# Prompt attention of a hybrid decoder layer: queries of the dilated patterns read in place, with a column step, instead of gathered into tiles

## The chip, the cores and the metric

The kernel runs on one core of one Trainium2 chip and computes one whole decoder layer for a prompt of 2048 tokens and for 64 sample tokens. The metric is device microseconds of one execution of the program. The median of three runs of the kernel before is 2801.09 us (2798.26 to 2801.12). Differences below about 0.2% can't be told from no change.

## The reference

The layer has two mixers side by side (attention in three dilated patterns, and a gated linear attention), a projection, and a feed-forward part with a convolution. Only the prompt attention matters here. Each of 8 heads (64 wide) attends in three patterns: window 128 and dilation 1, window 512 and dilation 4, window 2048 and dilation 16. Positions are split by their residue modulo the dilation, so that each pattern is a band of width 128 on strided subsequences. The three outputs are merged with weights proportional to their softmax denominators.

```python
PATTERNS = ((128, 1), (512, 4), (2048, 16))

def dilated_prompt(q, k, v, window, dil):
    ...
    n = window // dil
    span = n * dil
    ...
    def to_blocks(t):
        ...
        t = t.reshape(B, nb, n, dil, H, E)
        return t.transpose(0, 3, 4, 1, 2, 5)
    ...
    s = jnp.einsum('brhcie,brhcje->brhcij', qb, kk) * (E ** -0.5)
    ...
    s = jnp.where(mask, s, NEG)
    lse = jax.nn.logsumexp(s, axis=-1)
    p = jnp.exp(s - lse[..., None])
    o = jnp.einsum('brhcij,brhcje->brhcie', p, vv)
    ...

def prompt_attn(q, k, v):
    return combine_patterns([dilated_prompt(q, k, v, w, d) for w, d in PATTERNS])
```

## The kernel before

The program has three stages: the projections (`sweeps`), the prompt attention (`attention`), and the output projection with the feed-forward part (`tail`). The projections leave queries and keys in device memory, each split into a high and a low part (`qh`, `ql`, `kh`, `kl`), the queries in natural order of position, the keys in an order in which every block needed later consists of runs of 8 or 32 neighbouring columns.

`attention` goes through four pairs of heads. For each pair it walks the patterns 0, 1 and 2, and in each pattern four groups `g`. A group holds four blocks of 128 queries. In patterns 0 and 1 a group is two units of two blocks, in pattern 2 it is one unit of four blocks; so a pair has 20 units. For a pair, the tiles `aqs` (queries, one for each head, high and low part on the two halves of the partitions), `akh` and `akl` (keys) hold all 2048 positions; they come from two pools that alternate from pair to pair, and `at_load` fetches the next pair's on the SP queue while the present one is worked on. `at_loadv` fetches the values (`av`), also on SP.

A unit (`AtUnit`) has three steps. `qk_` computes the scores: for each block and head two matmuls into `pas`, with the queries as the stationary operand and 128 or 256 keys (high, then low part) as the moving one; DVE adds the mask and takes the row minimum (L1825; the queries carry a factor of -1/8), ACT takes the exponential (L1829). `t` transposes the weights on PE into `pat` (L1846), and ACT or DVE copies them to `apt` (L61, L63). `pv` multiplies with the values into `pao` (L1863), and DVE copies a finished group to `aop`. `drain` lets `t` run two units and `pv` three units behind `qk_`. The order on PE is fixed by `line` in `AtUnit`: each matmul is ordered behind the one recorded before.

In pattern 0 the 128 queries of a block are neighbours, and the stationary operand is a plain slice of `aqs`. In pattern 1 a block takes every 4th position, in pattern 2 every 16th. For these, `at_gather` copies the queries of a whole group, per head, into a tile `aqg` of 128 x 512 on POOL (L1128), two groups before they are used; there are five such tiles in the ring. `at_operands` then takes a slice of `aqg`.

When a pair's last unit is done, `at_merge` weights and adds its three patterns. It is a generator, moved on by one step per group of the next pair. Its bulk runs on POOL: for each of four column blocks, three multiplications of `aop` with the weights `awb` (L1227), two additions (L1212, L1237) and a store (L1239), behind DMAs that bring the weights in broadcast form (L1197, L1185). `aop` has five buffers, so that pattern 2 of the next pair is written into the buffer of this pair's pattern 0. The gathers and the merge stand in one fixed order on POOL, set by `Layer.line` (L1116); POOL executes it in order. The last pair is merged on PE, DVE, ACT and POOL together.

Of the kernel before, what the change touches and what calls it, by code (L numbers as in the profile page):

```python
# [11 lines left out]
F32R = mybir.dt.float32r  # L12
# [20 lines left out]
def cap(ap, off, dims):  # L33
    return bass.AP(tensor=ap.tensor, offset=ap.offset + off, ap=[list(ap.ap[0])] + [list(d) for d in dims])


class Layer:
# [369 lines left out]
    def sweep_a(self, c):  # L407
# [39 lines left out]
        for nn in range(2):  # L447
            wv = [self.wget(), self.wget()]
            for t0, m in self.vblocks(c):
                ps = self.psum.tile([128, 512], F32, name=self.n("pv"), tag="g1", bufs=3)  # L450
                self.vgemm(ps, xs, t0, m, wv)
                vs = self.st.tile([128, 256], F32, name=self.n("vs"), tag="vs", bufs=self.AB["vsb"])
                self.evac(vs[:m], ps[:m, :256], "v")
# [502 lines left out]
        yield  # L956


    AB = dict(mw=1, qg=5, vsb=5, mq='p', klh=1, q=2, v=6, s=6, pt=4, op=5, ps=3, ppt=2, po=2, am=1, skew=(2, 3), man=(), ea=3, ed=5, mp=12, aa=(1, 4, 7, 9, 10), ms='pppp', mv=2, em=1)

    def px(self, name, dt=F32):
        return self.pxpool.tile([128, 2 * H], dt, name=self.n(name), tag="px", bufs=4)
# [22 lines left out]
    def attention(self):  # L985
        with ExitStack() as ctx:
            self.aq[1] = self.pool(ctx, "at1")
            p = self.ap = self.pool(ctx, "at")
            self.app = self.pool(ctx, "atp", bass.MemoryType.PSUM)
            self.ev = 0  # L990
            pend = None
            fifo = []
            sk = self.AB["skew"]

            def drain(n):
                nonlocal pend
                if len(fifo) > sk[0]:
                    fifo[-1 - sk[0]].t()
                while len(fifo) > n:
                    un = fifo.pop(0)  # L1000
                    un.t()
                    un.pv()
                    if un.last:
                        for _ in pend or ():
                            pass
                        pend = self.at_merge(un.pr, un.ML, un.OP)

            if self.AB['man']:
                eng = mybir.EngineType
                ctx.enter_context(self.tc.manual_schedule(engines={getattr(eng, e) for e in self.AB['man']}))  # L1010
            self.vq = []
            self.at_loadv(0)
            self.at_loadv(1)
            for _ in self.at_load(0, ((1, 2),), to=self.qk0):
                pass
            rest = self.at_load(0, ((2, 4),), to=self.qk0)
            self.qgn = []
            for _ in range(self.AB["qg"]):
                p.tile([128, 4, 128], F32R, name=self.n("aqg"), tag="aqg", bufs=self.AB["qg"])
            for pat in range(3):  # L1020
                for _ in range(2):
                    p.tile([128, 16, 4], F32, name=self.n("aml"), tag=f"aml{pat}", bufs=2)
            for _ in range(2):
                p.tile([128, 3, 4, 128], F32, name=self.n("awb"), tag="awb", bufs=2)
            for _ in range(2):
                p.tile([128, 512], F32, name=self.n("amo"), tag="amo", bufs=2)
            pre = iter(())
            for pr in range(4):
                if pr == 3:
                    self.rctx.close()  # L1030
                    pre = self.wo_pre()
                qk = self.qk0
                nxt = self.at_load(pr + 1) if pr < 3 else iter(())
                ML, OP = [], []
                for pat in range(3):
                    base = 16 * (3 * pr + pat)
                    ml = p.tile([128, 16, 4], F32, name=self.n("aml"), tag=f"aml{pat}", bufs=2)
                    op = p.tile([128, 4, 512], F32, name=self.n("aop"), tag="aop", bufs=self.AB["op"])
                    ML.append(ml)
                    OP.append(op)  # L1040
                    for g in range(4):
                        if base // 4 + g + 2 < 48:
                            self.at_loadv(base // 4 + g + 2)
                        for _ in rest:
                            pass
                        po = [None]
                        nu = 1 if pat == 2 else 2
                        for u in range(nu):
                            fifo.append(AtUnit(self, pr, pat, g, u, nu, qk, base, ML, OP, po))
                            fifo[-1].qk_()  # L1050
                            drain(sk[1])
                            if pat:
                                next(pre, None)
                        if pend is not None:
                            next(pend, None)
                        if 5 <= 4 * pat + g < 11:
                            self.qk0 = next(nxt, self.qk0)
            for _ in pre:
                pass
            drain(0)  # L1060
            for _ in pend:
                pass
# [33 lines left out]
    def at_operands(self, qk, h, pat, g, blk):  # L1096
        QS, KH, KL = qk
        q, K = QS[h], (KH[h], KL[h])
        if pat == 0:
            idx = g * 4 + blk  # L1100
            lq = q[:, 128 * idx:128 * idx + 128]
            off = g * 512 + 8 * blk
            pst = 8 if blk else 488
            if idx == 0:
                return lq, [cap(k, off, [[32, 16], [1, 8]]) for k in K], [0], idx
            return lq, [cap(k, off - pst, [[pst, 2], [32, 16], [1, 8]]) for k in K], [idx - 1, idx], idx
        lq = self.qg[h][:, blk, :]
        if pat == 1:
            idx = g * 4 + blk
            if blk == 0:  # L1110
                return lq, [cap(k, 32 * g, [[128, 4], [1, 32]]) for k in K], [idx], idx
            return lq, [cap(k, (blk - 1) * 512 + 32 * g, [[512, 2], [128, 4], [1, 32]]) for k in K], [idx - 1, idx], idx
        idx = 4 * g + blk
        return lq, [cap(k, 32 * idx, [[512, 4], [1, 32]]) for k in K], [idx], idx

    def line(self, ins):  # L1116
# [2 lines left out]
            self.after(ins, self.atpo)  # L1119
        self.atpo = ins  # L1120
        return ins

    def at_gather(self, qk, pat, g):
        qg = []
        for h in range(2):
            t = self.ap.tile([128, 4, 128], F32R, name=self.n("aqg"), tag="aqg", bufs=self.AB["qg"])
            src = cap(qk[0][h], g, [[512, 4], [4, 128]]) if pat == 1 else cap(qk[0][h], 4 * g, [[1, 4], [16, 128]])
            self.line(self.nc.gpsimd.tensor_copy(t, src))  # L1128
            qg.append(t)
        self.qgn.append(qg)  # L1130

    def at_merge(self, pr, ML, OP):
        nc, p, pp, AB = self.nc, self.ap, self.app, self.AB
# [651 lines left out]
class AtUnit:  # L1785
# [13 lines left out]
    def qk_(self):  # L1799
        L = self.L  # L1800
        nc, p1, pp, AB = L.nc, L.aq[1], L.app, L.AB
        nbk = 4 // self.nu
        self.s = []
        if self.u == 0:
            if self.pat:
                L.qg = L.qgn.pop(0)
            n = 4 * self.pat + self.g + 2
            if 4 <= n < 12:
                L.at_gather(self.qk, n // 4, n % 4)
        scores = []  # L1810
        for h in range(2):
            ps = pp.tile([128, 512], F32, name=L.n("pas"), tag="as", bufs=AB["ps"])
            info = []
            scores.append((ps, info))
            for bb in range(nbk):
                lq, rk, keys, idx = L.at_operands(self.qk, h, self.pat, self.g, self.u * nbk + bb)
                nk = 128 * len(keys)
                sc = bb * (512 // nbk)
                for z in range(2):
                    self.line(nc.tensor.matmul(ps[:, sc:sc + nk], lq, rk[z], start=(z == 0), stop=(z == 1)))  # L1820
                info.append((self.u * nbk + bb, idx, sc, nk, keys))
        for h, (ps, info) in enumerate(scores):
            ssb = p1.tile([128, 512], F32, name=L.n("ass"), tag="ass", bufs=AB["s"])
            for blk, idx, sc, nk, keys in info:
                red = nc.vector.tensor_tensor_reduce(  # L1825
                    ssb[:, sc:sc + nk], ps[:, sc:sc + nk], L.amk[self.pat][:, 256 - nk:256],
                    scale=1.0, scalar=3e38, op0=ALU.add, op1=ALU.min, accum_out=self.ml[:, idx, h:h + 1])
            for blk, idx, sc, nk, keys in info:
                ex = nc.scalar.activation(ssb[:, sc:sc + nk], ssb[:, sc:sc + nk], AF.Exp, bias=self.ml[:, idx, h:h + 1],  # L1829
                                     scale=-1.0, accum_out=self.ml[:, idx, 2 + h:3 + h])  # L1830
            L.atl = ex, red
            self.s.append((ssb, info))
# [183 lines left out]
```

## Time and profile before

One execution was recorded by the profiler; times inside it count from the start of its span. PE is TensorE's matmuls and PEld its weight loads, DVE is VectorE, ACT is ScalarE, POOL is GpSimd, SP the engine that issues most DMAs.

| what | us |
|---|---|
| median of three runs | 2801.09 |
| span of the profiled execution | 2804.5 |
| first score matmul of the attention stage | 785.06 |
| first weight load of the output projection behind it | 1103.14 |
| first score load from `aqg` (pair 0, pattern 1) | 820.10 |
| POOL busy with the gathers (64 CASTs at L1128) | 69.0 |

The span is 3.4 us longer than the median of the runs. In the answers of the trace a row of a group reads: line, engine, operation, tile written <- tiles read, size x count, then busy time, mean ns of one, and the idle time before it with what ended it. In a timeline row the first two numbers are the start in us and the length in us. A table of stretches gives for each the busy time of each engine with its count of instructions, the granted TensorE clock (1.00 is full), the DMA share and GB/s.

### The profile page before, as it was taken

How to read it: one execution, taken by the hardware profiler on the slowest of the kernel's cores; microseconds unless marked ns; L12 is line 12 of the kernel's file. 1: busy time of each engine (PE TensorE's matmuls, PEld its weight loads, DVE VectorE, ACT ScalarE, POOL GpSimd, SP SyncE). 2: the span in 40 equal slices, each digit the busy share in tenths (PEclk: the TensorE clock that was granted, in tenths of full speed). 3: DMA queues.
4: the chain of work that ended last, by engine and by line, in shares of the span. 5: the costliest groups of instructions: out<-in, count | busy, mean ns of one | idle time of the engine just before them, and what ended most of it. 6: DMA issues, size and time to landing. Idle time of an engine off the chain costs nothing. (4 is left out here: it accounts for less than half of the span.)

```text
span 2804.5 us, 58656 instructions
## 1 busy us (share of the span) xinstructions
PE 2693.6 (96%) x22267; PEld 2540.2 (91%) x22267; DVE 1841.5 (66%) x4578; ACT 1267.8 (45%) x2959; POOL 590.0 (21%) x741
## 2 busy tenths in 40 slices
PE   7999999999989998998999999999999999999997
PEld 6788898888778787998899998999999999999997
DVE  6666655444347677466998888676567765666666
ACT  6535433333358776344554444443244433443332
POOL 3424243333333666013000012000020000200001
PEclk9999999999989989999999999999999999999998
DMA  7745536689798865367577677886598875876654
GB/s 293 259 173 178 177 108 215 253 328 374 262 222 171 190 159 152 106 216 261 192 276 287 232 261 291 287 298 236 204 330 282 297 244 200 324 255 215 221 188 149
DMA packets 283595, 656.83 MB, mean 234 GB/s; under 512 B 31841, under 2 KB 81633, under 8 KB 281265
## 3 DMA queue, kind: packets, MB, share of 16 engines
q1 hardware_dynamic: 253008, 574.66, 60.7%
q0 software_dynamic: 13216, 46.56, 5.1%
q10 hardware_dynamic: 17088, 31.86, 3.1%
q8 instruction: 176, 2.88, 0.4%
q14 instruction: 107, 0.87, 0.1%
HBM read 509.02 MB, written 143.94 MB: 233 GB/s over the span
## 5 line engine op out<-in xcount | busy, mean ns | idle before, releaser
L68 ACT ACTIVATE ws<-wr 128x512 fp32r<-128x512 f32 (+1 forms) x482 | 292.6, 616 | 431.5 <-PE pfe L1588 144.3
L90 PE MATMUL pfd<-hh,ws 128*128 128x264 f32 x2816 | 477.6, 286 | 6.7 <-ACT ws L68 5.0
L90 PEld LDWEIGHTS pfd<-hh,ws 128*128 128x128 f32 x2816 | 402.3, 190 | 9.1 <-ACT ws L68 6.7
L71 DVE TENSOR_TENSOR ws<-wr,ws 128x512 fp32r<-128x512 f32 (+1 forms) x482 | 319.2, 668 | 133.5 <-ACT ws L68 130.0
L90 PE MATMUL pfd<-hl,ws 128*128 128x264 f32 x1408 | 304.3, 286 | 0.1
L1588 PE MATMUL pfa<-xh,ws 128*128 128x264 f32 x1496 | 292.7, 286 | 7.7 <-ACT ws L68 3.3
L1588 PE MATMUL pfe<-xh,ws 128*128 128x264 f32 x1496 | 289.2, 286 | 3.8 <-DVE u L1575 1.9
L1588 PE MATMUL pfd<-xh,ws 128*128 128x264 f32 x1408 | 288.3, 285 | 3.8 <-DVE up L1575 2.9
L1588 PEld LDWEIGHTS pfa<-xh,ws 128*128 128x128 f32 x1496 | 237.1, 190 | 9.7 <-ACT ws L68 3.8
L1588 PEld LDWEIGHTS pfe<-xh,ws 128*128 128x128 f32 x1496 | 236.5, 189 | 4.5 <-DMA ws<-d_wst 2.3
L398 PE MATMUL pv<-wh,xh 128*128 128x256 f32 (+1 forms) x816 | 234.7, 288 | 1.1 <-DVE th L695 1.1
L1588 PEld LDWEIGHTS pfd<-xh,ws 128*128 128x128 f32 x1408 | 231.0, 189 | 4.6 <-DVE up L1575 3.4
L398 PE MATMUL pv<-wl,xh 128*128 128x256 f32 (+1 forms) x816 | 232.3, 285 | 0.0
L398 PE MATMUL pv<-wh,xl 128*128 128x256 f32 (+1 forms) x816 | 231.6, 284 | 0.0
L90 PEld LDWEIGHTS pfd<-hl,ws 128*128 128x128 f32 x1408 | 227.5, 190 | 0.4 <-DVE hl L71 0.4
L1537 POOL DMA_DIRECT2D xl<-d_xst x52 | 28.6, 550 | 903.0 <-PE pfe L1588 872.7
L1829 ACT ACTIVATE ass<-ass,aml 128x256 f32<-128x256 f32 (+1 forms) x384 | 173.6, 454 | 88.8 <-DVE aml L1825 87.5
L1588 PE MATMUL pfd<-xl,ws 128*128 128x264 f32 x704 | 200.6, 285 | 0.0
L90 PE MATMUL pq<-xh,wh 128*128 128x512 f32 (+2 forms) x480 | 175.5, 373 | 10.4 <-ACT xh L236 8.1
L1588 PE MATMUL pfe<-xl,ws 128*128 128x264 f32 x616 | 175.7, 285 | 0.0
L1588 PE MATMUL pfa<-xl,ws 128*128 128x264 f32 x616 | 175.1, 284 | 0.0
L90 PE MATMUL pq<-xl,wh 128*128 128x512 f32 (+2 forms) x480 | 174.4, 365 | 0.0
(341 smaller groups left out, 6624.0 us busy)
## 6 DMA issues: line engine op xcount, KB each, us to landing
ws<-d_wst SPq DMA_DIRECT2D x248, 512.0 KB
wr<-in_wu SPq DMA_DIRECT2D x114, 512.0 KB
d_wst<-ws SPq DMA_DIRECT2D x88, 512.0 KB
wr<-in_wd SPq DMA_DIRECT2D x160, 256.0 KB
wr<-in_wt SPq DMA_DIRECT2D x60, 512.0 KB
wh<-d_wbs SPq DMA_DIRECT2D x35, 512.0 KB
wl<-d_wbs SPq DMA_DIRECT2D x35, 512.0 KB
skp<-in_ckt SPq DMA_DIRECT2D x16, 1024.0 KB
```

The lines of the kernel that those rows point to most:

```text
L68: h = nc.scalar.activation(hi, src, AF.Copy)
L71: return h, (nc.gpsimd if lo_eng == "p" else nc.vector).tensor_tensor(lo, src, hi.bitcast(F32), op=ALU.subtract)
L90: mm = nc.tensor.matmul(o, ww[:, k, :], xx[:, s0:s0 + n], start=(k == order[0] and i == 0), stop=(k == order[-1] and i == 2))
L398: mm = nc.tensor.matmul(ps[:m, :256], x[:, t0:t0 + m], w[:, k % 4, :], start=(k == 0 and i == 0), stop=(k == KT - 1 and i == 2))
L1537: self.nc.gpsimd.dma_start(t.bitcast(F32), xo[i, z])
L1588: self.lastmm = nc.tensor.matmul(bank[:, :H], w[:, ww, k, :], xx, start=new and k == 0 and j == 0, stop=k == 3 and j == 2, skip_group_chec ...
L1829: ex = nc.scalar.activation(ssb[:, sc:sc + nk], ssb[:, sc:sc + nk], AF.Exp, bias=self.ml[:, idx, h:h + 1], scale=-1.0, accum_out=self.ml[: ...
```

## The change

The copies into `aqg` are dropped, with the tiles and the list that held them. `at_operands` builds the stationary operand of patterns 1 and 2 as an access pattern on `aqs` itself: 128 columns with a step of 4 or of 16 elements of 4 bytes. Pattern 0, the matmuls' order and number, the softmax, the values and the merge are as they were.

```diff
-        lq = self.qg[h][:, blk, :]
         if pat == 1:
             idx = g * 4 + blk
+            lq = cap(q, 512 * blk + g, [[4, 128]])
...
         idx = 4 * g + blk
+        lq = cap(q, idx, [[16, 128]])
         return lq, [cap(k, 32 * idx, [[512, 4], [1, 32]]) for k in K], [idx], idx
...
-    def at_gather(self, qk, pat, g):
-        qg = []
-        for h in range(2):
-            t = self.ap.tile([128, 4, 128], F32R, name=self.n("aqg"), tag="aqg", bufs=self.AB["qg"])
-            src = cap(qk[0][h], g, [[512, 4], [4, 128]]) if pat == 1 else cap(qk[0][h], 4 * g, [[1, 4], [16, 128]])
-            self.line(self.nc.gpsimd.tensor_copy(t, src))
-            qg.append(t)
-        self.qgn.append(qg)
...
-        if self.u == 0:
-            if self.pat:
-                L.qg = L.qgn.pop(0)
-            n = 4 * self.pat + self.g + 2
-            if 4 <= n < 12:
-                L.at_gather(self.qk, n // 4, n % 4)
```

`cap(t, off, dims)` is an access pattern on tile `t`: offset and (step, count) pairs along the free axis. Three places of the built programs show what this does to the order of instructions; numbers behind the names are the tiles' own and differ between the two programs, and the lines of the changed file are 3 to 17 smaller.

On PE, in pair 1 at the start of a unit of pattern 1, two output matmuls of an earlier unit and the first score matmuls of this one; `aqg` is the gathered tile. Before:

```order
L1863 MATMUL pao_11066<-apt_11015,av_10683 64x128
L1863 MATMUL pao_11066<-apt_11021,av_10683 64x128
L1820 MATMUL pas_11091<-akh_9995,aqg_10889 128x128
L1820 MATMUL pas_11091<-akl_10089,aqg_10889 128x128
L1820 MATMUL pas_11091<-akh_9995,aqg_10889 128x256
L1820 MATMUL pas_11091<-akl_10089,aqg_10889 128x256
```

And after, at the same place:

```order
L1846 MATMUL pao_11009<-apt_10958,av_10642 64x128
L1846 MATMUL pao_11009<-apt_10964,av_10642 64x128
L1803 MATMUL pas_11030<-akh_9970,aqs_9880 128x128
L1803 MATMUL pas_11030<-akl_10060,aqs_9880 128x128
L1803 MATMUL pas_11030<-akh_9970,aqs_9880 128x256
L1803 MATMUL pas_11030<-akl_10060,aqs_9880 128x256
```

Order and sizes are the same; only the second operand, the stationary one, is now the pair's whole query tile.

On POOL, where the merge of pair 1 begins in pair 2 (`awt`, `awb` the merge's weights, `aop` the pattern outputs). Before:

```order
L1128 COPY aqg_11697<-aqs_10979 128x512
L1128 COPY aqg_11699<-aqs_11254 128x512
L1197 DMA d_awd<-awt_11690 96x128
L1128 COPY aqg_11793<-aqs_10979 128x512
L1128 COPY aqg_11795<-aqs_11254 128x512
L1185 DMA awb_11883<-d_awd 64x1536 x2
L1128 COPY aqg_11893<-aqs_10979 128x512
L1128 COPY aqg_11895<-aqs_11254 128x512
L1185 DMA awb_11983<-d_awd 64x1536 x2
L1227 TENSOR_TENSOR aop_10365<-aop_10365,awb_11883 128x4x128
```

And after:

```order
L1186 DMA d_awd<-awt_11621 96x128
L1174 DMA awb_11806<-d_awd 64x1536 x2
L1174 DMA awb_11902<-d_awd 64x1536 x2
L1216 TENSOR_TENSOR aop_10328<-aop_10328,awb_11806 128x4x128
L1216 TENSOR_TENSOR aop_10737<-aop_10737,awb_11806 128x4x128
```

The merge's own instructions keep their order; the copies that stood before and between them are gone.

On SP, the queue of loads at the start of pair 2: the values of pair 2 (`av`), and queries and keys of pair 3. Before:

```order
L1088 DMA av_11330<-out_o_vp 128x1x128 x4
L1088 DMA av_11400<-out_o_vp 128x1x128 x4
L1076 DMA aqs_12084<-d_qh_60 64x4x512
L1076 DMA aqs_12084<-d_ql_64 64x4x512
L1076 DMA akh_12184<-d_kh_68 64x4x512 x2
L1076 DMA akl_12282<-d_kl_72 64x4x512 x2
L1076 DMA aqs_12359<-d_ql_64 64x4x512
L1076 DMA aqs_12359<-d_qh_60 64x4x512
L1076 DMA akh_12432<-d_kh_68 64x4x512 x2
L1088 DMA av_11471<-out_o_vp 128x1x128 x4
```

And after:

```order
L1085 DMA av_11261<-out_o_vp 128x1x128 x4
L1085 DMA av_11331<-out_o_vp 128x1x128 x4
L1073 DMA aqs_11999<-d_qh_60 64x4x512
L1073 DMA aqs_11999<-d_ql_64 64x4x512
L1085 DMA av_11402<-out_o_vp 128x1x128 x4
L1073 DMA akh_12095<-d_kh_68 64x4x512
L1085 DMA av_11495<-out_o_vp 128x1x128 x4
L1073 DMA akh_12095<-d_kh_68 64x4x512
L1073 DMA akl_12189<-d_kl_72 64x4x512
```

The next pair's keys, and the second head's queries, now stand behind value loads that they stood ahead of. The first load into an `aqs` buffer waited for POOL before, for the last gather from it; now it waits for PE, for the last score matmul that reads it.

More of the change, by code (lines that the diff above doesn't have):

```diff
@@ L956, in gla_sample @@
         yield
-    AB = dict(mw=1, qg=5, vsb=5, mq='p', klh=1, q=2, v=6, s=6, pt=4, op=5, ps=3, ppt=2, po=2, am=1, skew=(2, 3), man=(), ea=3, ed=5, mp=12, aa=(1, 4, 7, 9, 10), ms='pppp', mv=2, em=1)
+    AB = dict(mw=1, vsb=5, mq='p', klh=1, q=2, v=6, s=6, pt=4, op=5, ps=3, ppt=2, po=2, am=1, skew=(2, 3), man=(), ea=3, ed=5, mp=12, aa=(1, 4, 7, 9, 10), ms='pppp', mv=2, em=1)
     def px(self, name, dt=F32):
@@ L1016, in attention @@
             rest = self.at_load(0, ((2, 4),), to=self.qk0)
-            self.qgn = []
-            for _ in range(self.AB["qg"]):
-                p.tile([128, 4, 128], F32R, name=self.n("aqg"), tag="aqg", bufs=self.AB["qg"])
             for pat in range(3):
```

## The prediction

> **What bounds the kernel now.** I read the page first, for the engine that is busiest, then the busy time of each engine in stretches of the attention stage, then who waits for whom there.
>
> ```profile
> PE 2693.6 (96%) x22267; PEld 2540.2 (91%) x22267; DVE 1841.5 (66%) x4578; ACT 1267.8 (45%) x2959; POOL 590.0 (21%) x741
> ```
>
> PE leads over the whole span, and the gathers are on the least busy engine. But a share over the span says little about a stage. The change acts only in the attention stage, from the first score matmul at 784.94 us to about 1103 us. I cut this stage at the first weight load of each pattern, found in the timeline of weight loads. The rows below are pair 0 pattern 1 and 2, pair 1 pattern 0, 1 and 2, then patterns 1 and 2 of pairs 2 and 3.
>
> ```profile
> core 0: us, PE busy (x) PEld busy (x) DVE busy (x) ACT busy (x) POOL busy (x), PEclk, DMA share, GB/s
> 820.10:843.96 23.86, 23.86 (x249) 21.15 (x247) 17.05 (x74) 20.01 (x76) 8.48 (x8) 1.00 0.82 173
> 843.96:858.95 14.99, 14.99 (x156) 13.63 (x154) 10.94 (x70) 14.47 (x68) 5.57 (x6) 1.00 0.61 134
> 858.95:884.22 25.27, 25.21 (x261) 22.16 (x259) 23.43 (x99) 20.96 (x78) 2.75 (x3) 1.00 1.08 211
> 884.22:911.06 26.84, 24.34 (x248) 21.16 (x246) 17.15 (x74) 20.26 (x76) 15.12 (x16) 1.00 0.76 166
> 911.06:935.10 24.04, 20.02 (x157) 18.00 (x155) 10.81 (x70) 16.07 (x73) 23.09 (x24) 0.79 0.77 180
> ...
> 961.24:989.26 28.02, 25.81 (x248) 22.51 (x246) 17.24 (x74) 20.32 (x77) 17.86 (x21) 0.94 0.65 152
> 989.26:1012.41 23.15, 21.05 (x156) 18.86 (x154) 10.95 (x70) 16.35 (x74) 22.13 (x22) 0.72 0.65 166
> ...
> 1038.07:1062.05 23.98, 23.98 (x248) 21.11 (x246) 20.11 (x78) 22.19 (x79) 18.82 (x20) 1.00 0.85 181
> 1062.05:1085.10 23.05, 18.62 (x158) 16.98 (x156) 10.85 (x70) 16.34 (x75) 22.03 (x22) 0.85 0.50 124
> ```
>
> Two regimes stand here. In pair 0, PE is busy in all of 23.86 and 14.99 us: the stage is **bound by PE**, with ACT (14.47 of 14.99) close behind in pattern 2. In pattern 2 of pairs 1 to 3, POOL is busy in 23.09 of 24.04, 22.13 of 23.15 and 22.03 of 23.05 us. There the merge of the pair before and the gathers share POOL, and the same PE work (x156 to x158) takes 23 to 24 us instead of 15. The waits name it:
>
> ```profile
> POOL aqg L1128 <- PE pas L1820: 34.7, 7, 18.7
> ...
> PEld pas L1820 <- POOL aqg L1128: 15.8, 12, 3.0
> ...
> PE pas L1820 <- POOL aqg L1128: 13.0, 8, 2.8
> ```
>
> The last two are the same waits, seen by weight load and by matmul, so some 16 us of PE time. The first is POOL waiting for free tiles, mostly in pair 0, and costs nothing. The waits have a second price:
>
> ```profile
> 917.15 0.19 PEld L1820 LDWEIGHTS pas<-akh,aqg 128*128 128x128 f32 x1 [2.62 <-POOL aqg L1128]
> ...
> 918.62 0.33 PEld L1820 LDWEIGHTS pas<-akl,aqg 128*128 128x128 f32 x1
> 918.83 0.33 PEld L1820 LDWEIGHTS pas<-akh,aqg 128*128 128x128 f32 x1
> ```
>
> After a hole of 2.62 us the loads begin 0.21 us apart, about twice what stands below, and the granted clock over that pattern is 0.79 (0.72 and 0.85 in pairs 2 and 3; 1.00 in pair 0).
>
> **The change, part by part.** (1) *The gathers go.* 64 CASTs leave POOL, 69.0 us in all. PE no longer waits for them. What that gives back I read as the excess of pairs 1 to 3 over pair 0, which has the same PE work without a merge beside it. Pattern 1: 26.84, 28.02 and 23.98 less 23.86, so 2.98 + 4.16 + 0.12. Pattern 2: 24.04, 23.15 and 23.05 less 14.99, so 9.05 + 8.16 + 8.06. Together **32.5 us**, waits and lost clock both. What could be late next is the merge itself, since it frees the `aop` buffer into which pattern 2 of the next pair is written:
>
> ```profile
> 936.60 1.27 POOL L1212 TENSOR_TENSOR aop<-aop,aop 128x512 f32<-128x512 f32 x1
> ...
>   DVE aop L63: 0.8, 1
> ```
>
> The first row is the last use of the old buffer (pair 0's, 77.7 us after pair 1 began at 858.95); the second, from the view of that line, says that DVE waited for it only once, 0.8 us. Without gathers between them the merge steps move forward: 10 CASTs stood between 904 and 936 us, some 10 us, so that use comes about 67 us into the pair. Pattern 2's first result is written three groups after the pattern begins. With the slower loads below, that is about 25.3 + 30.5 + 3 x 5.4 = 72 us into the pair: 5 us of cover. If loads stay fast it is 25.3 + 23.9 + 3 x 3.7 = 60 us, 7 us too early; then DVE, and behind it PE, waits for the merge.
>
> (2) *512 weight loads read with a step.* Patterns 1 and 2 have 128 loads in each pair (16 blocks, two heads, high and low keys, two patterns), 512 in all; before they read 128 contiguous columns, now every 4th or every 16th fp32. What a contiguous load costs on the path is the distance of starts: first and last of 16 in a group of pattern 2, then first and last of 8 in a unit of pattern 1 whose matmuls have 256 columns:
>
> ```profile
> 851.24 0.19 PEld L1820 LDWEIGHTS pas<-akh,aqg 128*128 128x128 f32 x1 [0.17 <-POOL aqg L1128]
> ...
> 852.90 0.19 PEld L1820 LDWEIGHTS pas<-akl,aqg 128*128 128x128 f32 x1
> ...
> 899.59 0.19 PEld L1820 LDWEIGHTS pas<-akh,aqg 128*128 128x128 f32 x1 [0.17 <-issue]
> ...
> 900.42 0.19 PEld L1820 LDWEIGHTS pas<-akl,aqg 128*128 128x128 f32 x1
> ```
>
> That is 1.66 / 15 = 0.111 us and 0.83 / 7 = 0.119 us. In the first the matmul has 128 columns and in the second 256, yet the pace hardly differs: with 128 columns the load sets it, with 256 load and matmul are about level. So a dearer load falls on the path at once, since nothing beside it has slack.
>
> No row shows a stepped stationary read, so I bound it. Below: no dearer, 0; a gain has no reason, since the same 128 columns are loaded. Above: the nearest rows are stepped reads of the same 4-byte elements on other engines, each beside a plain operation of the same size.
>
> ```profile
> L68 ACT ACTIVATE ws<-wr 128x512 fp32r<-128x512 f32 x450 | 280.0, 630 | 422.5 <-PE pfe L1588 141.1 <-PE pfd L90 93.1 <-DMA wr<-in_wd 64.1
> ...
> L214 ACT COPY rbp<-rbn 128x512 f32<-128x512 f32 x4 | 4.3, 1070 | 0.0
> ...
> L1128 POOL CAST aqg<-aqs 128x512 fp32r<-128x512 f32 x64 | 69.0, 1107 | 47.2 <-PE pas L1820 34.7 <-DMA aqs<-d_ql 5.7 <-DMA aqs<-d_qh 5.4
> ...
> L1222 POOL TENSOR_SCALAR awb<-aaw 128x512 f32<-128x512 f32 x7 | 4.6, 668 | 0.3 <-PE pab L1224 0.3
> ```
>
> L214 reads every 16th element: 1070 against 630 ns, 0.86 ns more per element. The gathers (steps 4 and 16) take 1107 against 668 ns, also 0.86 ns. On both the element takes about twice its plain time, and the plain time, 0.111 us / 128 = 0.87 ns, is PE's as well. Between 0 and this I take the upper end, being nearest to two rows that agree: 128 x 0.86 = **0.110 us** more, 0.221 us for a load. Per pair, pattern 2 has 64 loads at +0.110 (7.0 us); pattern 1 has 16 at +0.110 and 48 that go from 0.119 to 0.221 (1.8 + 4.9 us). That is 13.7 us in a pair and **54.9 us** in four.
>
> [...]
>
> (3) *Other moves.* PE's order in the patterns is unchanged. SP's loads of the next queries now wait for PE instead of POOL:
>
> ```profile
> 856.97 0.60 SPq L1076 DMA_DIRECT2D aqs<-d_qh  x1
> ...
> 935.10 0.19 PEld L1820 LDWEIGHTS pas<-akh,aqs 128*128 128x128 f32 x1 [0.17 <-issue]
> ```
>
> These queries of pair 2 were issued 78 us before use, and their buffer's last reader on PE is done at about the same 857 us. Behind them on SP stand loads of keys (same lead) and of values, which now come two places earlier. I cost that at nothing; if the cover were gone, a wait of a few us per pair would show at the head of pattern 0. Some rows near the merge and in the tail swap places with neighbours: same instructions, 0, within 2 us either way.
>
> **Sum:** 54.9 - 32.5 = +22.4 us. The profiled execution has a span of 2804.5 us, 3.4 us above the median of 2801.1 us; both terms are differences inside this span, so I add them to the median: **2823 us**. Its own range, 50 to 56 us for the loads and 24 to 33 us given back, is 2818 to 2833, and I allow 2814.
>
> **Rivals.** *A stepped load costs nothing more.* PE's pace stays at 0.111 us, and what is given back decides: 32.5 us less the wait for the merge worked out above (7 us, of which PE's spare score and output buffers hide some 3) in three pairs, about 20 us. For it: PE streams 256 columns in the time in which it loads 128, so its port carries more than ACT's. Against it: two engines double alike. Time 2781, between 2768 (all given back) and 2790. It turns at a load dearer by 32.5 / 512 = 0.063 us: below that the change gains. *A price in between*, 0.03 to 0.09 us: 2790 to 2814. *The clock falls as well.* With matmuls further apart PE streams less per us; if that cost the clock as the 2.62 us hole did, the transposes and output matmuls of pattern 2 would take twice their time, about 2 us in each of 16 groups, +33: 2856. Against it: no hole is left, and pair 0 kept 1.00 in gapless groups. That the change doesn't do what it says is out: the order of the changed program has no gather and names `aqs` in these matmuls.
>
> **How the numbers follow.** Doubled loads 0.58, free 0.25, in between 0.10, clock too 0.07. A measurement of this kernel can tell about 0.2%, 5.6 us, from no change. Faster: the free case and 0.02 of the one between, 0.27. Same: 0.06 from the one between. Slower: 0.67. The range from 2775 to 2834 takes in nearly all of the likeliest, the case between and two thirds of the free one, 0.8; only the likeliest alone would have 2814 to 2833.
>
> **What would show it.** Distance of starts of score loads in patterns 1 and 2: 0.22 us (right), 0.11 (free). Pattern 1 of pair 0 near 30.5 us and pattern 2 near 22 us, and the same length in all four pairs, with clock 1.00; no PE wait for POOL. If pattern 2 still differs between pair 0 and the others, the merge bounds it and my 32.5 is too large. Wrong outright would be a load of 0.11, or one beyond 0.3.

## The result, and the profile after

The changed kernel takes **2839.94 us** (median of 4 runs, 2837.52 to 2842.51) against 2801.11 us (2798.26 to 2808.07) for the kernel before in the same series: a ratio of 1.0145 with a 95% interval of 1.0132 to 1.0158. It is slower by 38.8 us. The prediction said slower, 2823 us, in a range up to 2834; the time lies above the range.

The first row of the page of the changed kernel answers to the one quoted from before:

```profile
PE 2744.6 (97%) x22267; PEld 2593.8 (91%) x22267; DVE 1844.9 (65%) x4578; ACT 1272.9 (45%) x2959; POOL 522.5 (18%) x677
```

As many matmuls as before, PE 51.0 us busier, POOL 67.5 us less. The table of stretches, cut at the first score load of each pattern, shows where. Rows: pattern 1 and 2 of pair 0, then of pairs 1, 2 and 3; the columns are those of the table in the prediction.

```profile
813.33:844.74 31.41, 31.41 (x248) 28.70 (x246) 17.95 (x74) 20.62 (x76) 0.00 (x0) 1.00 0.81 174
844.74:870.45 25.71, 25.71 (x157) 23.87 (x155) 10.98 (x70) 16.73 (x74) 0.00 (x0) 0.80 0.22 58
...
895.69:927.11 31.42, 31.42 (x248) 28.71 (x246) 17.87 (x74) 20.58 (x76) 14.79 (x16) 1.00 0.86 197
927.11:954.40 27.29, 27.29 (x156) 24.75 (x154) 11.08 (x70) 16.74 (x74) 16.97 (x17) 0.64 0.40 105
...
980.05:1011.46 31.41, 31.41 (x248) 28.70 (x246) 17.87 (x74) 20.56 (x76) 15.54 (x17) 1.00 0.80 190
1011.46:1037.63 26.17, 26.17 (x157) 24.26 (x155) 11.06 (x70) 16.85 (x74) 16.22 (x16) 0.80 0.45 132
...
1062.87:1094.29 31.42, 31.42 (x248) 28.71 (x246) 21.51 (x78) 23.10 (x80) 23.83 (x25) 1.00 0.81 202
...
1094.30:1120.10 25.80, 25.80 (x172) 24.04 (x170) 11.58 (x71) 16.69 (x73) 8.63 (x8) 0.87 0.12 42
```

PE is busy in every microsecond of these eight stretches. Pattern 1 takes the same 31.41 or 31.42 us in all four pairs: nothing waits for POOL any more, and the 23.86 of pair 0 before has grown by 7.55 us. Pattern 2 takes 25.7 to 27.3 us instead of the 22.0 forecast, and the column behind POOL says why: the granted clock is 0.64 to 0.87, without a hole. The timeline of weight loads gives their pace. Shown are the first and last load of a unit of pattern 1, eight transposes (L1829) at full clock, the first and last load of a group of pattern 2, eight transposes at a clock of 0.50, and a group of pattern 2 in pair 1 at a clock of 0.50:

```profile
825.89 0.31 PEld L1803 LDWEIGHTS pas<-akh,aqs 128*128 128x128 f32 x1 [0.17 <-issue]
...
827.51 0.33 PEld L1803 LDWEIGHTS pas<-akl,aqs 128*128 128x128 f32 x1
...
842.87 0.90 PEld L1829 LDWEIGHTS pat<-c_ident,ass 128*128 128x128 f32 x8
...
844.74 0.29 PEld L1803 LDWEIGHTS pas<-akh,aqs 128*128 128x128 f32 x1 [0.17 <-issue]
...
848.02 0.31 PEld L1803 LDWEIGHTS pas<-akl,aqs 128*128 128x128 f32 x1
...
853.65 1.57 PEld L1829 LDWEIGHTS pat<-c_ident,ass 128*128 128x128 f32 x8
...
940.31 0.29 PEld L1803 LDWEIGHTS pas<-akh,aqs 128*128 128x128 f32 x1 [0.33 <-issue]
...
943.56 0.31 PEld L1803 LDWEIGHTS pas<-akl,aqs 128*128 128x128 f32 x1
```

A stepped load costs 1.62 / 7 = 0.231 us in pattern 1 and 3.28 / 15 = 0.219 us in pattern 2, against 0.119 and 0.111 before. At half clock the pace is the same, 3.25 / 15 = 0.217 us: these loads do not follow the clock. The transposes do: a block of eight takes 0.90 us at full clock and 1.57 us at half. Contiguous score loads do too, 0.111 us apart at full clock and 0.21 us at 0.50, behind the hole in the prediction's rows. Cutting pattern 2 of pair 0 at its groups shows when the clock goes:

```profile
844.74:850.10 5.36, 5.36 (x40) 5.03 (x38) 2.41 (x18) 4.26 (x20) 0.00 (x0) 1.00 0.27 77
850.10:856.70 6.60, 6.60 (x39) 6.09 (x37) 2.85 (x18) 4.48 (x21) 0.00 (x0) 0.74 0.14 40
856.70:863.60 6.90, 6.90 (x43) 6.40 (x41) 2.56 (x17) 4.20 (x19) 0.00 (x0) 0.75 0.00 0
...
940.30:943.80 3.50, 3.50 (x18) 3.49 (x16) 0.93 (x8) 1.07 (x6) 3.34 (x4) 0.50 0.00 0
```

The first group is as long as forecast (5.4 us) at full clock; from the second on each loses 1.2 to 1.5 us (the fourth takes 6.85). The last row is the stretch of loads in pair 1. Cut finer, the clock is 1.00 or 0.50 in the traces of both kernels, and here it changes every 3.41 us, with PE busy throughout:

```profile
849.41:852.83 3.42, 3.42 (x29) 3.25 (x23) 2.39 (x12) 1.52 (x9) 0.00 (x0) 1.00 0.13 38
852.83:856.24 3.41, 3.41 (x19) 3.08 (x20) 1.16 (x12) 3.20 (x16) 0.00 (x0) 0.50 0.13 38
856.24:859.65 3.41, 3.41 (x23) 3.24 (x20) 0.86 (x8) 1.37 (x6) 0.00 (x0) 1.00 0.00 0
```

The stage went from 318.2 us (784.94 to 1103.14) to 360.7 us (779.01 to 1139.71), +42.5. Outside it the two profiled executions differ by -5.9 us ahead and -1.5 us behind, which the change doesn't touch; the profiles of all the kernels below have their first score load between 777.7 and 780.5 us too, so it was the recorded execution of before that came late to the stage. The terms, in us:

| term | predicted | measured |
|---|---|---|
| excess of pairs 1 to 3 in patterns 1 and 2 | -32.5 | -32.5 |
| dearer loads, pattern 1 | +26.7 | 4 x 7.55 = +30.2 |
| dearer loads, pattern 2 | +28.2 | 4 x 64 x 0.108 = +27.6 |
| lower clock in pattern 2 | 0 | 104.97 - 4 x 14.99 - 27.6 = +17.4 |
| pattern 0 and the end of the stage | 0 | -1.8 + 1.6 = -0.2 |
| sum | +22.4 | +42.5 |

The cut behind pattern 2 of pair 3 does not fall on the same instruction in both traces: that stretch holds 158 matmuls before and 172 after. At 0.11 us each (0.90 / 8), some 1.5 us of the 17.4 may belong to the row below it; this is an estimate.

### The profile page after: what moved, and what is told of

It reads as the page before. It is cut to its first block, busy times and chain, and to the rows that moved or that the text cites. A ratio compares the mean times of both kernels' runs of the same rounds, so it can differ in the third digit from the quotient of the medians.

```text
span 2839.6 us, 58521 instructions
## 1 busy us (share of the span) xinstructions
PE 2744.6 (97%) x22267; PEld 2593.8 (91%) x22267; DVE 1844.9 (65%) x4578; ACT 1272.9 (45%) x2959; POOL 522.5 (18%) x677
## 5 line engine op out<-in xcount | busy, mean ns | idle before, releaser
L1808 DVE CUSTOM_DVE_ANT_0 ass<-pas,atab 128x256 f32<-128x256 f32 (+1 forms) x384 | 120.6, 361 | 102.9 <-PE pas L1803 92.5
```

The source lines that it names most:

```text
L1808: red = nc.vector.tensor_tensor_reduce(ssb[:, sc:sc + nk], ps[:, sc:sc + nk], L.amk[self.pat][:, 256 - nk:256], scale=1.0, scalar=3e38, op ...
```

## Experiments

Ratios are to the kernel before, run beside each, with the 95% interval. "Plain" below is the kernel of the first experiment; `lq` is the stationary operand.

**The step alone.** The changed kernel with neighbouring columns read instead of stepped ones.

```diff
-            lq = cap(q, 512 * blk + g, [[4, 128]])
+            lq = q[:, 512 * blk:512 * blk + 128]
...
-        lq = cap(q, idx, [[16, 128]])
+        lq = q[:, 128 * idx:128 * idx + 128]
```

> The changed kernel with the step taken out: patterns 1 and 2 read 128 neighbouring columns of the query tile as stationary operand, so the scores are those of other queries; matmuls, order and everything else are the same. It parts the two terms of my sum, gathers gone and stepped loads. Theory A (the loads cost what the trace of the changed kernel shows, 0.22 us instead of 0.11): load distance back at 0.111 us, clock 1.00 in pattern 2, and the time falls below the kernel before by what the missing gathers give back. If all 32.5 us come back: 2769 us. Theory B (the merge holds pattern 2 of pairs 1 to 3 once the gathers are gone): about 2781 us, with DVE waiting several us for POOL's addition into aop (L1201). Theory C (the waits for gathers were cover for something else): about 2801 us.

Measured: 2783.72 us, ratio 0.9959 (0.9937 to 0.9981), with the wait for the merge that Theory B names. The ten runs spread from 2779.56 to 2798.88 us, six of them below 2786 and four above 2793. So the whole loss hangs on the step, 56.2 us between the medians of the two kernels, and without gathers the stage is not free either. Its stretches (pattern 2 of pair 1, pattern 0 of pair 2), and the waits of DVE in its timeline, behind pairs 1 and 2:

```profile
902.70:920.70 18.00, 18.00 (x156) 16.48 (x154) 10.91 (x70) 13.11 (x62) 16.78 (x18) 0.82 0.86 200
920.70:948.83 28.13, 25.74 (x261) 22.16 (x259) 23.27 (x98) 20.90 (x78) 7.57 (x8) 1.00 0.81 187
```

```profile
924.75 1.07 DVE L63 COPY aop<-pao 128x512 f32<-128x512 f32 x1 [4.22 <-POOL aop L1201]
...
995.72 1.07 DVE L63 COPY aop<-pao 128x512 f32<-128x512 f32 x1 [7.06 <-POOL aop L1201]
```

DVE waits 4.22 and 7.06 us for the buffer that the merge still holds: the wait that the prediction put at 7 us for fast loads. With slow loads it is gone, also as forecast.

**One pattern at a time.** First pattern 1 stepped and pattern 2 gathered on POOL as before, then the reverse.

```diff
-        lq = cap(q, idx, [[16, 128]])
+        lq = self.qg[h][:, blk, :]
...
+            if self.pat == 2:
+                L.qg = L.qgn.pop(0)
+            n = 4 * self.pat + self.g + 2
+            if 8 <= n < 12:
+                L.at_gather(self.qk, n // 4, n % 4)
```

> Pattern 1 read with a step of 4, pattern 2 gathered on POOL as before. Theory A (both steps cost the same per load, the clock loss belongs to pattern 2 alone): pattern 1 at 31.4 us in all four pairs with clock 1.00, against 102.7 us together in the kernel before, so +23 us; pattern 2 with half the gathers on POOL between 15 and 20 us per pair, against 85.2 us together, so 5 to 20 us less. 2805 to 2819 us. Rival B (a step of 16 bytes is cheap and only the step of 64 bytes costs): load distance 0.12 us in pattern 1 and a time below 2795 us.

> Pattern 1 gathered on POOL as before, pattern 2 read with a step of 16. Theory A (price of the load and of the clock in pattern 2): pattern 1 near 24 us in all pairs (96 against 102.7 us before), pattern 2 at 25.5 to 27.5 us in each pair with clock 0.6 to 0.9 (105 against 85.2 us): about +13 us, 2814 us. Theory B (only the loads' own price counts, the clock is noise of one execution): pattern 2 at 22 us and 2798 us.

With pattern 2 gathered: 2810.96 us, ratio 1.0034 (1.0022 to 1.0046), inside Theory A's range, though made up otherwise: pattern 2 is back at 15.0 us in pairs 0 to 2, and pattern 1 of pairs 2 and 3 takes 33.2 and 34.1 us. With pattern 1 gathered: 2829.02 us, ratio 1.010 (1.008 to 1.012), 15 us above the 2814 expected. The stretches of that second kernel, pattern 2 of the four pairs:

```profile
838.02:864.46 26.44, 26.44 (x156) 24.43 (x155) 11.13 (x70) 16.85 (x74) 0.00 (x0) 0.81 0.45 106
...
920.95:945.34 24.39, 24.39 (x156) 22.39 (x154) 10.98 (x70) 16.59 (x74) 20.96 (x20) 0.87 0.59 143
...
997.88:1024.98 27.10, 27.10 (x156) 25.09 (x154) 11.07 (x70) 16.84 (x74) 21.07 (x20) 0.75 0.64 166
...
1076.14:1104.00 27.86, 27.86 (x168) 26.02 (x168) 11.07 (x70) 16.94 (x75) 16.37 (x16) 0.75 0.30 77
```

Together 105.8 us, as Theory A has it (105), and 17.8 us more than four times the 22.0 at full clock. The miss lies elsewhere: against the expectation pattern 1 is 7.5 us longer, nearly all of it in pair 1 (31.19 us), and against the kernel before pattern 0 of pairs 1 to 3 is 3.5 us longer and the end of the stage 2.9 us. In pattern 1 of pair 1 the gathers stand on POOL behind the merge, which waits for its weights, and PE then waits 4.3 us for a gather:

```profile
POOL aop L1228 <- DMA awb<-d_awd: 8.2, 1, 8.2
```

The lost clock (0.75 to 0.87 here) belongs to stepped loads in pattern 2, whose matmuls have 128 columns, and not to those in pattern 1, most of which have 256 (1.00 in all pairs of the changed kernel).

**More columns beside the same loads.** In three of four blocks of pattern 2, 256 columns are streamed instead of 128. The first version is

```diff
-        return lq, [cap(k, 32 * idx, [[512, 4], [1, 32]]) for k in K], [idx], idx
+        return lq, [cap(k, 32 * idx, [[512, 4], [1, 64 if blk < 3 else 32]]) for k in K], [idx], idx
...
+                    nw = 256 if self.pat == 2 and bb < 3 else nk
```

which, other than its text says, takes other keys in those three blocks; the second has `[[32, 2], [512, 4], [1, 32]]` there, so that the block's own 128 keys come first.

> The changed kernel, with 256 instead of 128 moving columns in three of four score blocks of pattern 2; the extra columns are overwritten by the next block, the result is the same. The stepped load takes 0.22 us, and 256 columns stream in 0.11 us, so nothing gets longer by itself; only PE streams more per us. Theory A (the granted clock falls in pattern 2 because little streams while the loads take twice as long): clock 1.00 in pattern 2, groups of 5.4 us instead of 6.5 to 6.9, pattern 2 near 22 us in each pair, some 17 us in all: about 2823 us. Theory B (the clock falls for another reason, such as waits between groups, or the step itself): clock 0.64 to 0.87 there as now and 2840 us.

> The changed kernel in which three of the four pattern-2 score blocks of each group stream 256 moving columns instead of 128: the block's own 128 keys first, and 128 more whose scores the next block overwrites, so that the result is that of the changed kernel. It repeats the run with wider streams, which had taken other keys. Theory A, the granted clock falls in pattern 2 because the array streams too little beside the long loads: with more streams under the same loads the clock stays at 1.00, pattern 2 takes 22.0 us in each pair instead of 25.7, 27.3, 26.2, 25.8, and the time is about 2824. Theory B, the stepped reads lower the clock whatever streams beside them: pattern 2 stays at 25 to 27 us and the time at about 2840.

Measured: 2824.34 us, ratio 1.0085 (1.0058 to 1.0111), and 2826.09 us, ratio 1.0095 (1.0075 to 1.0114): 14 to 16 us less than the changed kernel, for doing more. Pattern 2 of pairs 0 and 1 in the second, and then its stage from within pattern 0 of pair 0 to behind pattern 2 of pair 3:

```profile
846.21:868.24 22.03, 22.03 (x156) 20.68 (x154) 10.70 (x70) 15.47 (x69) 0.00 (x0) 1.00 0.21 59
...
924.90:946.92 22.02, 22.02 (x156) 20.67 (x154) 10.89 (x70) 15.83 (x72) 16.81 (x17) 1.00 0.50 133
...
806.20:1113.30 307.10, 304.94 (x2543) 277.13 (x2541) 201.31 (x916) 217.90 (x828) 99.69 (x103) 1.00 0.66 157
```

The stepped loads are all there, and the clock stays at 1.00 in all four pairs: Theory A. In pairs 0 to 2 pattern 2 is 13.1 us shorter, added up, than in the changed kernel.

**Few columns beside contiguous loads.** The other side of the same question, on the plain kernel, with 16 and then with 128 columns:

```diff
+                if self.pat == 2:
+                    for z in range(2):
+                        self.line(nc.tensor.matmul(ps[:, sc:sc + 16], lq, cap(self.qk[1][h], 32 * idx, [[1, 16]]), start=True, stop=True))
```

> The changed kernel with contiguous stationary reads (patterns 1 and 2 score other queries than the reference's), and in pattern 2 each pair of score matmuls is preceded by two more with the same stationary operand that stream 16 columns each, whose scores are overwritten. So a group of pattern 2 has 32 contiguous loads of 0.111 us, as long on the path as 16 stepped ones of 0.22 us, with nearly as few columns streamed beside them as in the changed kernel, and no column step. Question: does the granted clock fall because of the step, or because PE streams little in its busy time? Without a lower clock a pattern 2 takes 14.98 + 64 x 0.111 = 22.1 us. Theory A, it is the streams: granted clock between 0.6 and 0.9 in pattern 2 and 24 to 28 us a pattern, as in the changed kernel (25.7 to 27.3). Theory B, it is the step: clock 1.00 and 22.1 us. Time about 2812 by A and 2800 to 2806 by B, since part of the waits for the merge is covered in both.

> The same with 128 instead of 16 columns in the extra matmuls: as many contiguous loads, but each with a full stream beside it. Control for the run with short ones. Both theories: clock 1.00 and about 22.1 us in pattern 2 of each pair, time 2800 to 2806. If pattern 2 is longer than that at clock 1.00, the extra matmuls have another price than their loads, and the run with short ones is to be read against this one.

Measured: 2829.77 us (2814.51 to 2834.30, ratio 1.0097, 1.0064 to 1.0130) with short, 2806.73 us (ratio 1.0022, 0.9999 to 1.0044) with long matmuls. Pattern 2 of pairs 0, 1 and 2 with short ones, in the shortest of the four runs:

```profile
838.35:863.66 25.31, 25.31 (x221) 23.47 (x219) 10.97 (x70) 16.56 (x74) 0.00 (x0) 0.87 0.50 117
...
912.97:947.32 34.35, 34.35 (x220) 32.03 (x218) 10.97 (x70) 16.34 (x73) 21.68 (x20) 0.62 0.67 162
...
996.98:1020.71 23.73, 23.73 (x221) 22.21 (x219) 10.89 (x70) 16.57 (x74) 21.31 (x20) 0.93 0.72 183
```

And the same stretches with long ones, with pattern 1 of pair 2 ahead of its pattern 2:

```profile
838.10:860.22 22.12, 22.12 (x220) 20.77 (x218) 10.70 (x70) 15.47 (x70) 0.00 (x0) 1.00 0.47 114
...
910.32:932.45 22.13, 22.13 (x220) 20.78 (x218) 10.89 (x70) 14.87 (x68) 20.97 (x20) 1.00 0.75 185
...
957.73:985.58 27.85, 24.14 (x248) 21.12 (x246) 17.06 (x74) 21.43 (x80) 15.20 (x17) 1.00 0.93 201
985.58:1012.52 26.94, 26.94 (x221) 25.26 (x219) 11.06 (x70) 14.36 (x66) 16.52 (x16) 0.81 0.58 156
```

No step is left, and the clock still falls where the matmuls are short (0.87, 0.62 and 0.93): Theory A. Full streams hold it at 1.00 in pairs 0 and 1; in pair 2 it falls behind a pattern 1 in which PE had 3.7 us of holes (24.14 busy of 27.85), and 26.94 us follow at 0.81. The last holes stand right before the fall:

```profile
982.64:986.05 3.41, 1.49 (x16) 1.08 (x17) 0.00 (x0) 0.41 (x2) 3.25 (x4) 1.00 0.65 133
986.05:996.29 10.24, 10.24 (x56) 9.58 (x56) 3.57 (x19) 3.30 (x16) 8.54 (x9) 0.50 0.76 176
```

So in these traces the clock halves behind two kinds of stretch: one with holes (1.49 us busy of 3.41 above), and one in which PE loads more than it streams (loads 0.219 us apart beside 128 columns in the changed kernel). The 34.35 us in pair 1 with short matmuls are more than Theory A's 28; the clock stays at half there for 27.3 us on end, and what holds it there is not shown. The median is 18 us above its 2812, and the three longer runs were not traced.

**How the price goes with the step.** Steps of 2 and 3 elements in place of 4 and 16.

```diff
-            lq = cap(q, 512 * blk + g, [[4, 128]])
+            lq = cap(q, 512 * blk + g, [[2, 128]])
...
-        lq = cap(q, idx, [[16, 128]])
+        lq = cap(q, idx, [[3, 128]])
```

> The changed kernel with smaller column steps: the stationary operand is read at a step of 2 elements (8 bytes) in pattern 1 and of 3 elements (12 bytes) in pattern 2, so both patterns score other queries than the reference's. Question: does a stepped weight load cost by the fact of a step, or by how far it steps? In the changed kernel the distance of two loads is 0.231 us at a step of 4 elements (pattern 1) and 0.219 us at 16 (pattern 2), and with contiguous reads 0.119 and 0.111. [...] Theory B, by the fact of a step: 0.231 and 0.219 again, patterns of 31.4 and 25 to 27 us, time about 2840. [...]

Measured: 2794.47 us, ratio 0.998 (0.9967 to 0.9993), faster than Theory B has it. Its weight loads, a unit of pattern 1 and a group of pattern 2:

```profile
826.29 0.19 PEld L1803 LDWEIGHTS pas<-akh,aqs 128*128 128x128 f32 x1 [0.17 <-issue]
...
827.14 0.20 PEld L1803 LDWEIGHTS pas<-akl,aqs 128*128 128x128 f32 x1
...
837.70 0.25 PEld L1803 LDWEIGHTS pas<-akh,aqs 128*128 128x128 f32 x1 [0.17 <-issue]
...
840.32 0.27 PEld L1803 LDWEIGHTS pas<-akl,aqs 128*128 128x128 f32 x1
```

Step 2 gives 0.85 / 7 = 0.121 us, where contiguous loads took 0.119. Step 3 gives 2.62 / 15 = 0.175 us, between the contiguous 0.111 and the 0.219 of step 16. So the fact of a step alone does not set the price: over the contiguous pace it is 0.002 us a load at step 2, 0.064 at step 3, 0.112 at step 4 and 0.108 at step 16. From 4 to 16 it does not grow. What makes it so is not shown.

**Versions meant to beat both.** Two gather everything in pair 0 and a part of the rest (here the first; the second gathers all of pattern 1 and head 0 of pattern 2, with the wide streams on head 1), and two make gathers of pairs 1 to 3 on DVE.

```diff
+    def gath(self, pr, pat, g, h):
+        return pr == 0 or (pat == 1 and g < 3) or (pat == 2 and h == 0)
...
-            self.line(self.nc.gpsimd.tensor_copy(t, src))
+            self.line((self.nc.vector if h and pr else self.nc.gpsimd).tensor_copy(t, src))
```

> A mixture of the two kernels, meant to beat both: GpSimd gathers everything in pair 0, and in pairs 1 to 3 the groups 0 to 2 of pattern 1 and head 0 of pattern 2; group 3 of pattern 1 and head 1 of pattern 2 are read with the column step. So 8 + 16 stepped loads more in each of three pairs (pattern 1: 16 loads of group 3, pattern 2: 32 loads of head 1: 144 in all), and 18 of the 64 gathers fewer. Theory A: the 32.5 us that pairs 1 to 3 lose to late gathers come back in good part once GpSimd has 6 gathers of 1.107 us fewer in each pair, against 144 x 0.110 = 15.8 us of loads: 6 to 16 us faster than before, 2785 to 2794. Theory B: the gathers that are left still come late and the loads are paid besides: no change or slower, 2800 to 2815.

(Its count of loads in a pair is 16 in group 3 of pattern 1 and 32 in head 1 of pattern 2; the total of 144 stands.)

> Another mixture: GpSimd gathers everything in pair 0, all of pattern 1, and head 0 of pattern 2 in pairs 1 to 3; head 1 of pattern 2 in pairs 1 to 3 is read with the column step, and three of its four score blocks stream 256 moving columns (the further 128 scores are overwritten), which is to keep the clock up. That is 96 stepped loads and 12 gathers fewer. Theory A: 96 x 0.110 = 10.6 us of loads against more than that of the 32.5 us of waits: 4 to 14 us faster than before, 2787 to 2797. Theory B: what waits in pairs 1 to 3 is the merge's share of GpSimd, and 12 gathers fewer do not clear it: 2800 to 2812.

> The kernel before, with all gathers kept (contiguous loads of 0.111 and 0.119 us) but shared: in pairs 1 to 3 those of head 1 go from GpSimd to VectorE, which is busy 17 of 24 to 28 us in pattern 1 and 11 of 15 to 24 us in pattern 2. Question: were late gathers the whole reason of the 32.5 us that pairs 1 to 3 took longer than pair 0? Theory A, GpSimd was short of time for merge and gathers, and 8 gathers fewer in a pair (24 in all, 27 us of its time) free it; VectorE takes 24 x about 0.6 us beside PE: 8 to 16 us faster than before, 2784 to 2792, near the run with contiguous reads of other queries (2783.7), which has no gather at all. Theory B, VectorE stands in the way of mask and minimum and copies, so that PE waits for it instead: no change or slower, 2798 to 2815.

> As the shared version, but in pairs 1 to 3 VectorE makes all 16 gathers of a pair, so GpSimd does nothing but the merge there, as in the changed kernel, while the weight loads stay contiguous. Theory A, what is left is the merge alone: the time of the run with contiguous reads of other queries, 2784, plus up to 6 us because 8 x 0.6 us more on VectorE in pattern 2 (11 + 5 of 15 us) leave it little slack: 2784 to 2792. Theory B, VectorE becomes late in pattern 2: patterns of 17 us and more in each pair, 2795 to 2810.

Measured: 2795.03 us, ratio 0.9985 (0.9971 to 0.9998); **2792.01 us, ratio 0.9973 (0.9961 to 0.9984)**; 2795.56 us, 0.9992 (0.9983 to 1.0002); 2795.36 us, 0.9989 (0.9973 to 1.0006). Of the four only the second is faster by more than 0.2%, as its Theory A has it, and its interval reaches down to 0.16%. The first ends just above its Theory A, and the two with gathers on DVE miss theirs by 3 us and more; their intervals include no change at all. The trace of the first is of its longest run (2806.67 us). Below stand what PE waited for most between 806 and 1082 us, and then a stretch of 3.41 us shortly before pattern 2 of pair 2, and that pattern:

```profile
PE pao L1871 <- DMA av<-out_o_vp: 10.8, 5, 4.5
```

```profile
986.80:990.21 3.41, 0.66 (x8) 0.42 (x8) 0.01 (x2) 2.16 (x8) 3.04 (x4) 1.00 0.26 74
...
992.04:1018.22 26.18, 26.18 (x156) 23.86 (x154) 11.07 (x70) 14.46 (x66) 17.41 (x16) 0.58 0.53 138
```

The same pattern in the second:

```profile
985.67:1004.14 18.47, 18.47 (x156) 17.12 (x154) 10.89 (x70) 15.80 (x72) 17.53 (x18) 1.00 0.74 174
```

In the first, PE waits for no gather there but for the loads of the values, and the clock halves at 990.21, behind that hole and before the pattern begins. So the low clock of this pattern starts from a hole, and the two rows do not show what the wide streams do in the mixture. With all gathers of pairs 1 to 3 on DVE the late gathers are gone (pattern 2 of pair 1 below takes 15.78 instead of 24.04 us), but pattern 0 behind it grows from 26.14 to 31.97 us:

```profile
903.31:919.09 15.78, 15.45 (x156) 13.64 (x154) 14.86 (x80) 14.21 (x65) 15.23 (x15) 1.00 0.81 198
919.09:951.06 31.97, 27.88 (x261) 23.75 (x259) 26.02 (x99) 22.19 (x82) 9.83 (x10) 0.95 0.97 215
```

```profile
925.51 2.04 DVE L63 COPY aop<-pao 128x512 f32<-128x512 f32 x2 [4.36 <-POOL aop L1212]
```

It is the merge again, 4.36 of the 5.83 us. A gather on DVE, a group in the table of lines, also takes more than the 0.6 us that the author had estimated:

```profile
L1128 DVE CAST aqg<-aqs 128x512 fp32r<-128x512 f32 x48 | 47.4, 1007 | 0.0
```

## Why the prediction was wrong

1. **What the gathers cost** (-32.5 us): right in size. Pairs 1 to 3 have pair 0's length in pattern 1, and no hole in pattern 2. The merge did not come in the way, by the cover that the prediction worked out; in the plain kernel it did. One part was put down to the wrong wait: in pattern 1 of pair 2 of the kernel before (4.16 us of the excess) PE waited for the loads of the values, and for no gather. That this wait went as well is luck, as far as shown:

```profile
PE pao L1863 <- DMA av<-out_o_vp: 2.2, 2, 1.3
```

2. **The price of a stepped load** (0.221 us, from ACT and POOL): right to 1% in pattern 2 (0.219), 4% low in pattern 1 (0.231), because a load with 256 columns beside it had been 0.119 and not 0.111 to begin with and the price comes on top of that. This is 3.5 us of the miss. (The 54.9 us are 54.8 by their own factors, 4 x 13.7.)
3. **The clock** (put at nothing): wrong, and this is the step that failed. "The clock falls as well" stood among the rivals with a chance of 0.07 and a price of 33 us; against it the prediction held that "no hole is left, and pair 0 kept 1.00 in gapless groups". Gapless is not enough. The kernel loses 16 to 17.4 us this way, about half of the rival's price, since the first group of a pattern 2 in pair 0 still runs at 1.00 and the stepped loads themselves, more than half of each group, do not slow down (0.217 us apart at 0.50, 0.219 at 1.00). Full streams beside the same loads bring the clock back (1.00 in pattern 2), and short streams beside contiguous loads lose it (0.62 to 0.93): so in these runs few streamed columns beside long loads lower it, with or without a step. PE's busy time doesn't show this: its matmul records fill every microsecond of pattern 2, whether the clock is full or half.
4. **Queues and order** (0): right within the 2 us that the prediction allows. Pattern 0 is 1.8 us shorter and the end of the stage 1.6 us longer; that only 0.2 us remain is luck.

The warning was in the rows: a load of 0.22 us beside a matmul of 128 columns, which the row of 256 columns bounds at 0.06 us, leaves PE streaming for 27% of the score phase, against 54% before (estimates from these rows). At step 3 it is 34%, and the clock stayed at 1.00 in pairs 0 and 2; in pair 1 (0.92) it halved once, behind a stretch with a hole. The fourteen traces, of both kernels and the twelve experiments, allow a count. Take the stretches of 3.41 us of the stage, from 800 to 1125 us, in which the clock is full and PE has no hole, and count the columns streamed in each (two output matmuls of 64 columns that start 0.006 us apart as one). Half clock followed 29 of them, and none of these streamed more than 2304 columns; full clock followed 981, and only three of these streamed that few. The wide streams put the number at 3200 and more in pattern 2. The count is not the whole rule: at half clock, 1792 to 2176 columns were followed by either clock.

In the attention stage of both traces, before and after, the clock keeps each value for 3.41 us or a multiple of it, and in pattern 2 of the changed kernel it fell without an idle gap of PE. What exactly lowers it stays open. So does the length of the end of the stage where gathers remain.

With the loads at 57.8 us, the change loses 25 us before the clock takes 16 to 17 more; it would break even at 32.5 / 512 = 0.063 us more for a load.

## What to carry to other kernels

Before a copy is replaced by a strided stationary read, measure the distance of the loads at its own step: here a step of 2 fp32 was free (0.121 against 0.119 us), 3 cost 0.06 us a load, and 4 and 16 cost 0.11 us, all of it on the path beside matmuls of 128 and of 256 columns. Look at the granted clock as a separate term wherever loads grow against streams, since here a gapless PE row didn't protect it (0.64 to 0.87 in pattern 2); widening the streams was cheaper than the lost clock, by 14 us. And where one engine carries two late jobs, as POOL carries gathers and merge, taking one away gave back only up to the other: 16 us here between the medians (2799.86 to 2783.72; 11 us by the ratio), not 32.5.

## What had not been expected

- Streaming twice the columns, half of them thrown away, made the changed kernel 14 us faster between the medians (2839.94 to 2826.09).
- Stepped loads keep their pace at half clock: 0.217 us at 0.50, 0.219 at 1.00.
- A step of 2 elements costs nothing that can be seen (0.121 against 0.119 us).
- In the plain kernel a gapless pattern with contiguous loads still ran at 0.82 (18.00 us instead of 14.98). Its clock had halved at 902.30 us, behind 3.41 us in which PE was busy for 1.32 us.
- In the first mixture the longest waits of PE were not for gathers but for the loads of the values (10.8 us).
- The stepped copy on DVE took 0.90 us in the shared version and 1.01 us in the other, nearly POOL's 1.1.
